# The first store of a pooling kernel in five pieces instead of one

## The chip, the cores and the metric

The kernel runs on one core of a Trainium2 chip. The metric is the time of one execution in microseconds, as the device measures it; before the change the median of three runs is 394.51 us (394.41 to 395.09). A profiled execution gives a trace, whose span begins and ends with the core's first and last instruction.

## The reference

The input `x` is 32 x 256 x 4096 in fp32, 134 MB. Along the last axis, each group of four neighbours gives one output, the root of the mean of the squares (an Lp pooling with p = 2 and kernel size 4); the output is 32 x 256 x 1024, 33.6 MB.

```python
for i in range(out_length):
    window = np.abs(x[:, :, 4 * i:4 * i + 4]) ** 2.0
    result[:, :, i] = (np.mean(window, axis=-1)) ** 0.5
```

## The kernel before

Both tensors are seen as flat. The input is cut into 20 loads of 128 partitions; loads 0 to 18 have W = 13184 values per partition (52,736 bytes), load 19 has 11648. Three tiles `x_tiles` take them in turn, so load i + 3 goes into the slot of load i. SP issues all loads (line 84): the first three at the start, then load i + 3 at the end of the work on load i.

The work on a load: ACT squares each half in place (`square`, line 98), DVE adds pairs (`pairs`, line 104) and then twos of these (`fours`, line 108) into one of two PSUM tiles `s_tiles`, and ACT takes the root of a quarter into `o_tile` (`root`, line 111). The order on ACT is by hand: the roots of load i - 1 stand between the two squares of load i.

Loads are grouped into blocks, [0, 1, 2, 3], [4, 5, 6, 7], [8, 9, 10, 11], [12, 13], [16, 17, 14, 15], [18] and [19], and a block is one contiguous stretch of the output. `o_tile` holds 4 x R values a partition, R = W / 4 = 3296, that is a block of four loads. There is one `o_tile`, so the roots of a block's successor wait until the block's store has landed. For this reason, where load i - 1 is the first of a block (i = 5, 9, 13, 17), both squares of load i come first, then the roots of load i - 1; DVE adds the pairs of both halves first and the fours, which need free PSUM tiles, last.

ACT issues the stores of blocks 0 to 3, right behind the last roots (line 95); SP issues those of blocks 4, 5 and 6 at the end. A store of a full block is one DMA of 128 partitions x 52,736 bytes.

At the very start ACT issues five tiny copies, one for each of the blocks 0 to 4 (`touch`, line 121): 128 values of every eighth partition's row from the input into the same rows of the block's output, which the block's store overwrites later.

Of the kernel before, what the change touches and what calls it, by code (L numbers as in the profile page):

```python
# [1 line left out]

# [4 lines left out]


@with_exitstack
def kernel(  # L10
    ctx: ExitStack,
    tc: tile.TileContext,
    x: bass.AP,
    p: float,
    kernel_size: int,
    out: bass.AP,
):

    nc = tc.nc

    assert float(p) == 2.0, "kernel specialized for p == 2"
    k = int(kernel_size)  # L30
    assert k == 4, "kernel specialized for kernel_size == 4"

    P = nc.NUM_PARTITIONS
    fp32 = mybir.dt.float32
    Act = mybir.ActivationFunctionType
    add = mybir.AluOpType.add
    xf = x.rearrange("b c l -> (b c l)")
    of = out.rearrange("b c l -> (b c l)")
    total = xf.shape[0] // P

    W = 13184
    H, R = W // 2, W // k
    X_SLOTS = 3
    TOUCH = 128
    LAST = total - 19 * W
    widths = [W] * 19 + [LAST]
    n = len(widths)
    assert 0 < LAST <= W and LAST % 16 == 0


    blocks = [[0, 1, 2, 3], [4, 5, 6, 7], [8, 9, 10, 11], [12, 13], [16, 17, 14, 15], [18], [19]]
    block_of = {i: b for b, loads in enumerate(blocks) for i in loads}
    block_width = [sum(widths[i] for i in loads) for loads in blocks]

    x_pool = ctx.enter_context(tc.tile_pool(name="x_pool", bufs=1))
    o_pool = ctx.enter_context(tc.tile_pool(name="o_pool", bufs=1))
    s_pool = ctx.enter_context(tc.tile_pool(name="s_pool", bufs=1, space=bass.MemoryType.PSUM))
    x_tiles = [x_pool.tile([P, W], fp32, name=f"xt{j}") for j in range(X_SLOTS)]
    o_tile = o_pool.tile([P, 4 * R], fp32, name="ot")
    first = o_pool.tile([P, 1], fp32, name="first")  # L60
    s_tiles = [s_pool.tile([P, 2048], fp32, name=f"st{j}") for j in range(2)]
    ctx.enter_context(tc.manual_schedule())

    def rows(flat, b, div):
        at = sum(block_width[:b]) * P // div
        return flat[at:at + block_width[b] * P // div].rearrange("(p w) -> p w", p=P)


    place = {}
    for b, loads in enumerate(blocks):  # L70
        for q, i in enumerate(loads):
            if i < 18:
                place[i] = o_tile[:, q * R:(q + 1) * R]
    free = x_tiles[17 % X_SLOTS]
    place[18] = free[:, 0:R]
    place[19] = free[:, R:R + LAST // k]

    xs = {}

    def load(i):  # L80
        b = block_of[i]
        at = sum(widths[j] for j in blocks[b][:blocks[b].index(i)])
        xs[i] = x_tiles[i % X_SLOTS][:, 0:widths[i]]
        nc.sync.dma_start(out=xs[i], in_=rows(xf, b, 1)[:, at:at + widths[i]])  # L84

    def store(b, queue):
        if b <= 2:
            held = o_tile[:, :]
        elif b == 3:
            held = o_tile[:, 0:2 * R]  # L90
        elif b == 4:
            held = o_tile[:, :]
        else:
            held = place[blocks[b][0]]
        queue.dma_start(out=rows(of, b, k), in_=held)

    def square(v):
        nc.scalar.activation(out=v, in_=v, func=Act.Square)  # L98

    def pairs(v):  # L100

        q = v.rearrange("p (n j) -> p n j", j=k)
        h = v[:, 0:v.shape[1] // 2].rearrange("p (n j) -> p n j", j=2)
        nc.vector.tensor_tensor(out=h, in0=q[:, :, 0:2], in1=q[:, :, 2:4], op=add)  # L104

    def fours(o, v):
        h = v[:, 0:v.shape[1] // 2].rearrange("p (n j) -> p n j", j=2)
        nc.vector.tensor_tensor(out=o, in0=h[:, :, 0], in1=h[:, :, 1], op=add)  # L108

    def root(o, s):  # L110
        nc.scalar.activation(out=o, in_=s, func=Act.Sqrt, scale=1.0 / k)  # L111

    def roots(i):
        for c in range(2):
            root(place[i][:, c * R // 2:(c + 1) * R // 2], s_tiles[c][:, 0:R // 2])
        if i in (3, 7, 11, 13):
            store(block_of[i], nc.scalar)

    def touch(b):
        to = rows(of, b, k)[0:P:8, 0:TOUCH]  # L120
        nc.scalar.dma_start(out=to, in_=rows(xf, b, 1)[0:P:8, 0:TOUCH])

    for b in range(5):
        touch(b)
    for i in range(X_SLOTS):
        load(i)

    nc.vector.memset(first[:, :], 1.0)  # L128
    root(first[:, :], first[:, :])
    for i in range(18):  # L130
        halves = [xs[i][:, c * H:(c + 1) * H] for c in range(2)]
        waits = i > 1 and (i - 1) % 4 == 0
        square(halves[0])
        if i and not waits:
            roots(i - 1)
        square(halves[1])
        if waits:
            roots(i - 1)
            for v in halves:
                pairs(v)  # L140
            for c, v in enumerate(halves):
                fours(s_tiles[c][:, 0:R // 2], v)
        else:
            for c, v in enumerate(halves):
                pairs(v)
                fours(s_tiles[c][:, 0:R // 2], v)
        if i + X_SLOTS < n:
            load(i + X_SLOTS)
    roots(17)


    c = 5560
    v = xs[18][:, 0:c]
    nc.vector.tensor_tensor(out=v, in0=v, in1=v, op=mybir.AluOpType.mult)  # L154
    square(xs[18][:, c:W])
    store(4, nc.sync)
    for a, b in ((0, c), (c, W)):
        pairs(xs[18][:, a:b])
        fours(place[18][:, a // k:b // k], xs[18][:, a:b])
    ends = [0, 6912, 10064, LAST]  # L160
    for a, b in zip(ends, ends[1:]):
        v = xs[19][:, a:b]
        o = place[19][:, a // k:b // k]
        square(v)
        if a == 0:
            root(place[18], place[18])
            store(5, nc.sync)
        pairs(v)
        fours(o, v)
        if a:  # L170
            root(*last)
        last = (o, o)
    root(*last)
    store(6, nc.sync)


# [1 line left out]
_INS = ['x', 'p', 'kernel_size']  # L178
_OUTS = [((32, 256, 1024), 'float32')]

_NUMBERS = {'p': 2.0, 'kernel_size': 4}


# [26 lines left out]
```

## Time and profile before

| | before |
|---|---|
| median of three runs | 394.51 us |
| profiled execution | 394.68 us |
| its span | 392.9 us |
| ACT busy | 279.3 us (71%) |
| DVE busy | 223.3 us (57%) |
| DMA moved | 167.83 MB, mean 427 GB/s |
| DMA queue 1 (SP) | 3312 packets, 144.15 MB |
| DMA queue 10 (ACT) | 736 packets, 23.67 MB |
| first store issued, landed | 90.15 us, 127.44 us |

Busy time is that in which an engine runs an instruction; instructions that issue DMAs aren't counted. The page cuts the span into 40 equal slices of 9.8 us and gives for each the mean busy share of the 16 DMA engines in tenths and the GB/s that they moved. Queue 1 is fed by SP, queue 10 by ACT, and both run on the same 16 DMA engines. A DMA row of the page gives the time from the issue to the landing, when its completion is signalled.

### The profile page before, as it was taken

Reading aid. Unit: us, or ns where it says so; the run is one execution under the profiler, and the core shown is the slowest. Engines: PE = TensorE matmul, PEld = TensorE weight load, DVE = VectorE, ACT = ScalarE, POOL = GpSimd, SP = SyncE. Lnnn points to the kernel's source line nnn. Section 1 sums busy time; section 2 is a strip of 40 time slices with the busy share of each in tenths; the row PEclk is TensorE's granted clock in tenths of the full one; section 3 lists DMA queues with packets and bytes.
Section 4 is the critical chain, followed back from the end, with each engine's and each line's share of the span. In section 5 each row is a group of like instructions: output and inputs, shape, how many; then the busy total and the mean of one; then the engine's idle time right before and its main releaser. Section 6 shows DMA issues by size and latency. Waiting matters only on the chain.

```text
span 392.9 us, 318 instructions
## 1 busy us (share of the span) xinstructions
DVE 223.3 (57%) x84; ACT 279.3 (71%) x82; POOL 0.2 (0%) x4
## 2 busy tenths in 40 slices
DVE  0046586666460568664606666645066654769992
ACT  1095988987650999886419898774297929897792
POOL 0000000000000000000000000000000000000000
DMA  8999999999999999999999999999999999999997
GB/s 344 432 430 430 430 430 435 456 440 387 430 430 430 430 430 440 435 451 435 440 430 431 440 430 435 435 435 430 435 430 419 440 430 430 430 434 446 425 423 320
DMA packets 4050, 167.83 MB, mean 427 GB/s; under 512 B 512, under 2 KB 592, under 8 KB 592
## 3 DMA queue, kind: packets, MB, share of 16 engines
q1 hardware_dynamic: 3312, 144.15, 85.3%
q10 hardware_dynamic: 736, 23.67, 13.9%
q14 instruction: 2, 0.02, 0.0%
HBM read 134.26 MB, written 33.60 MB: 427 GB/s over the span
## 4 chain that ended last, share of the span: by engine, by line
DMA 73%; ACT 17%; DVE 6%; issue 2%; SPq 0%; ACTq 0%; DVEq 0%
DMA xt<-in_x_dram 46%; DMA out_dram<-ot 27%; ACT xt L98 12%; ACT ot L111 5%; DVE xt L104 3%; DVE st L108 2%; DVE xt L108 1%; ACT xt L111 1%; SPq L84 0%; ACTq L98 0%; DVEq L104 0%; ACTq L111 0%
## 5 line engine op out<-in xcount | busy, mean ns | idle before, releaser
L98 ACT ACTIVATE xt<-xt 128x6592 f32<-128x6592 f32 (+4 forms) x40 | 221.4, 5547 | 58.5 <-DMA xt<-in_x_dram 56.8
L104 DVE TENSOR_TENSOR xt<-xt 128x3296 f32<-128x3296 f32 (+5 forms) x41 | 143.0, 3489 | 125.2 <-ACT xt L98 124.9
L108 DVE TENSOR_TENSOR st<-xt 128x1648 f32<-128x1648 f32 x36 | 67.4, 1882 | 36.2 <-ACT ot L111 34.3
L111 ACT ACTIVATE ot<-st 128x1648 f32<-128x1648 f32 x36 | 53.5, 1536 | 43.3 <-DMA out_dram<-ot 40.5
L108 DVE TENSOR_TENSOR xt<-xt 128x1390 f32<-128x1390 f32 (+4 forms) x5 | 7.3, 1452 | 0.2
L111 ACT ACTIVATE xt<-xt 128x3296 f32<-128x3296 f32 (+3 forms) x4 | 6.0, 1492 | 1.1 <-DVE xt L108 1.1
L154 DVE TENSOR_TENSOR xt<-xt 128x5560 f32<-128x5560 f32 x1 | 5.9, 5943 | 0.0
L111 ACT ACT_TABLE_LOAD x1 | 1.3, 1283 | 4.0 <-issue 4.0
L128 DVE MEMSET first<- 128x1 f32 x1 | 0.1, 59 | 0.8 <-PEq L191 0.8
L111 ACT ACTIVATE first<-first 128x1 f32<-128x1 f32 x1 | 0.2, 203 | 0.0
L191 POOL MEMSET const-bfloat16-1.0<- 128x1 bf16 x1 | 0.1, 102 | 0.0
L191 POOL MEMSET const-uint8-127<- 128x1 uint8 x1 | 0.1, 102 | 0.0
L191 POOL MEMSET const-float32-0.0<- 128x1 f32 x1 | 0.1, 99 | 0.2 <-issue 0.2
L191 POOL MEMSET const-float32-1.0<- 128x1 f32 x1 | 0.1, 99 | 0.0
## 6 DMA issues: line engine op xcount, KB each, us to landing
xt<-in_x_dram SPq DMA_DIRECT2D x19, 6592.0 KB, 33.6
out_dram<-ot ACTq DMA_DIRECT2D x3, 6592.0 KB, 35.2
out_dram<-ot SPq DMA_DIRECT2D x1, 6592.0 KB, 24.8
xt<-in_x_dram SPq DMA_DIRECT2D x1, 5824.0 KB, 25.2
out_dram<-ot ACTq DMA_DIRECT2D x1, 3296.0 KB, 27.4
out_dram<-xt SPq DMA_DIRECT2D x1, 1648.0 KB, 10.5
out_dram<-xt SPq DMA_DIRECT2D x1, 1456.0 KB, 5.8
out_dram<-in_x_dram ACTq DMA_DIRECT2D x5, 8.0 KB, 15.2
```

The source lines that it names most:

```text
L98: nc.scalar.activation(out=v, in_=v, func=Act.Square)
L104: nc.vector.tensor_tensor(out=h, in0=q[:, :, 0:2], in1=q[:, :, 2:4], op=add)
L108: nc.vector.tensor_tensor(out=o, in0=h[:, :, 0], in1=h[:, :, 1], op=add)
L111: nc.scalar.activation(out=o, in_=s, func=Act.Sqrt, scale=1.0 / k)
L128: nc.vector.memset(first[:, :], 1.0)
L154: nc.vector.tensor_tensor(out=v, in0=v, in1=v, op=mybir.AluOpType.mult)
L191: nc = _bacc.Bacc("TRN2", target_bir_lowering=False, num_devices=1)
```

## The change

The store of block 0 goes out as five DMAs, all issued by ACT in one go. Four take partitions 0 to 15: columns 0 to 824, 824 to 2472, 2472 to 5768 and 5768 to 13184, so 3.3, 6.6, 13.2 and 29.7 KB of each partition's row. The fifth takes partitions 16 to 127 with whole rows. Of the five tiny copies only that into block 4 is left. The other stores, the loads and the work on ACT and DVE stay as they are, in the same order.

```diff
         if i in (3, 7, 11, 13):
-            store(block_of[i], nc.scalar)
+            (store if i > 3 else ramp)(block_of[i], nc.scalar)
+
+    def ramp(b, queue):
+
+        cuts = [0, R // 4, 3 * R // 4, 7 * R // 4, 4 * R]
+        for a, e in zip(cuts, cuts[1:]):
+            queue.dma_start(out=rows(of, b, k)[0:16, a:e], in_=o_tile[0:16, a:e])
+        queue.dma_start(out=rows(of, b, k)[16:P], in_=o_tile[16:P, :])
...
-    for b in range(5):
-        touch(b)
+    touch(4)
     for i in range(X_SLOTS):
         load(i)
```

## The prediction

> **What bounds the kernel now.** I read the page's slices first, to see whether any engine or only the DMA is full.
>
> ```profile
> DVE 223.3 (57%) x84; ACT 279.3 (71%) x82; POOL 0.2 (0%) x4
> ...
> DMA  8999999999999999999999999999999999999997
> GB/s 344 432 430 430 430 430 435 456 440 387 430 430 430 430 430 440 435 451 435 440 430 431 440 430 435 435 435 430 435 430 419 440 430 430 430 434 446 425 423 320
> ```
>
> The 16 DMA engines are full from the first slice to the last, at 430 GB/s; ACT and DVE have slack. So a change gains or loses only what it adds to or takes from DMA time, idle DMA time included. In the trace's records of single DMA packets each 52,736-byte row of a load or store takes 1.947 us and the next starts 1.944 us after it, from 1.7 us to 391 us on every engine. Two places differ on every engine: its very first row (2.5 to 3.2 us), and one row per engine near 92 us, where slice 10 falls to 387 GB/s. Busy time in short windows there (window, length, engines' busy time, clock, DMA share, GB/s):
>
> ```profile
> 90.00:92.00 2.00, 1.90 (x2) 1.57 (x2) 0.00 (x0) 1.00 0.98 422
> 92.00:94.00 2.00, 0.87 (x1) 2.00 (x1) 0.00 (x0) 1.00 1.50 422
> 94.00:96.00 2.00, 0.00 (x0) 2.00 (x1) 0.00 (x0) 1.00 0.97 422
> ```
>
> Sixteen rows start in each window. Those of 92 to 94 us have a share of 1.50, so 3.0 us each instead of 1.95: the first store, issued at 90.15, costs every engine a stall of 1.06 us on average (0.54 to 1.76). The stores at 169.20 and 247.24 show none. This stall is what the change can win.
>
> Then the chain of waits around that store (start, length, what):
>
> ```profile
> 90.15 37.29 DMA out_dram<-ot
> ...
> 127.52 1.55 ACT ot L111
> ...
> 130.89 1.89 DVE st L108
> ...
> 132.79 27.73 DMA xt<-in_x_dram
> ```
>
> The roots of load 4 overwrite `o_tile`, so ACT waits until the whole first store has landed (127.44). Behind that stand the sums of load 5 and the issue of load 8 (132.79), which takes load 5's slot. Meanwhile loads 6 and 7 keep the DMA busy. How long? The timeline of ACT and DVE:
>
> ```profile
> 144.97 5.70 ACT L98 ACTIVATE xt<-xt 128x6592 f32<-128x6592 f32 x1 [0.43 <-DMA xt<-in_x_dram]
> 148.20 1.88 DVE L108 TENSOR_TENSOR st<-xt 128x1648 f32<-128x1648 f32 x1
> ...
> 160.60 5.70 ACT L98 ACTIVATE xt<-xt 128x6592 f32<-128x6592 f32 x1 [1.49 <-DMA xt<-in_x_dram]
> ```
>
> Load 7 lands at about 144.95, load 8 at 160.52. Load 9 is issued after the sum that ends at 150.08, which is 22.64 us after the store's landing, with no wait on a load between (ACT and DVE run back to back from 127.52). So a later landing of the first store delays loads 8 and 9 one for one, against a cover of about 12 and 10 us.
>
> Last, how small DMAs share the engines with loads: the tiny copies' time to landing.
>
> ```profile
> DMA to landing us min/median/max: 8.6/15.2/19.7
> ```
>
> They are issued 0.61 us apart from 0.73 on, so the first lands at 9.3 and the third at 17.2: 3.9 us per copy of 512 bytes a row, two load rows. The packet records show why: an engine takes the two queues in turn, and a DMA's completion is a packet of its own. The order is copy, load row, completion, load row, next copy.
>
> **Four tiny copies go.** Each costs an engine 24 + 6 ns (packet and completion), so 4 x 0.03 = -0.12 us. They need not be missed: the stores at 378 and 386 us go to parts of the output no tiny copy touched, and their rows run at 493 and 436 ns for a quarter of the bytes, without a stall. Their ACT issues (4 x 0.61) lay under ACT's 13.65 us wait for the first load.
>
> **Four more issues on ACT at 90.15.** At 0.34 (a store) to 0.61 us (a tiny copy) these are 1.4 to 2.4 us. Behind them on ACT stands the square of load 4's second half, then DVE's sums and load 7's issue (101.87 becomes 104.3 at most). ACT waits 5.55 us before 101.80 and load 7's first row has its turn near 129, so nothing shows; uncovered it would be 2.4 us. In the changed instruction order the second piece waits for the one tiny copy left (long landed), and loads 9 to 11 wait for pieces done some 50 us earlier: nothing.
>
> **The store lands later.** Per engine the store was 8 rows and a completion, 9 turns; between the first and the last lie 8 turns of the load queue, 7 rows and one load completion. Now it is four pieces, each with a completion, then 7 rows and a completion: 16 turns, with 15 load turns between, of which two are load completions. Bytes stored are equal, so the landing moves by 13 - 7 = 6 load rows: 6 x 1.944 = 11.7 us, to 139.1. Bytes are not lost by this, but the loads run out: load 8's issue moves to 144.4 and its first packet, 0.85 us later (the last store on idle engines: issued 386.24, first packets 387.1), to 145.3, against 144.6 when the slowest engine is done with load 7. Load 9 is issued at 161.7, first packet 162.6; load 8's last row ended at 160.2 before. Together the DMA loses 162.6 - 160.2 = 2.4 us. I take 2.3, since the slowest engines lose a little less. Load 10 (issue near 175.9, needed at 178.1) is in time again. The lag of ACT behind the loads, 9.7 us at load 8, shrinks by some 1.4 us a load, for ACT needs 14.15 us for a load that takes 15.55; store 1 goes out near 179, load 12 at 219.4 against 224.7 when the queue would be empty. Loads 18 and 19, and with them the end, keep only the 2.3 us.
>
> Bounds: if no engine is late with its first piece and the stall stays, the landing is 136.9 (the stores at 169.20 and 247.24 landed in 35.15 and 34.99 us, the first in 37.29) and load 9's first packet 160.4: about 0. A rerun of 37.29 gives 2.3. I take 2.3, the row of this very store.
>
> **What a piece costs.** No row shows 16 engines reading 16 neighbouring partitions. Lower bound: by bytes, 0.12 + 0.24 + 0.49 + 1.10 = 1.95 us, the row they replace, and the stall gone: -1.06. Upper bound: all eight row-equivalents of the store at the 3.0 us of the 92 us row: 8 x 1.06 = +8.5. I take the stall as it was plus one row at 3.0: +1.06, as the nearest row is a store's first. The 112-partition DMA I take as before, 7 rows an engine.
>
> [...]
>
> **Sum.** The profiled execution took 394.68 us, its span 392.9, 1.8 around it; the median of three runs is 394.51, so the steps are added to that: 394.51 - 0.12 + 2.3 + 1.06 = 397.7.
>
> **The rivals.**
> Rival 1, faster: the small pieces take the stall away and the loads do not run dry. It decides if the store lands by 160.2 - 0.85 - 22.64 = 136.7 or the alternation is looser than the tiny copies show. For it: the stall falls only on the first store, and the first piece is a sixteenth of a row. Against: the stalled row is a load's, before the store's first row, so its size may not matter. 394.51 - 0.12 - 1.06 = 393.3.
> Rival 2, no change: the change does not do what it says, the stall comes whatever the piece's size, and the landing is 136.9: 394.4 to 394.7.
> Rival 3, much slower: 16 neighbouring partitions, or 112 split by sevens, are read slowly at four to seven of the eight turns (+4.2 to +7.4), with the run-dry of 2.3: 401 to 404; without it 399.
>
> **How the numbers follow.** My forecast 0.43 (own range 395.4 to 399.5), rival 3 0.27, rival 2 0.15, rival 1 0.15. A measurement of this kernel can tell about 0.2%, 0.8 us. Faster is rival 1, 0.15; within 0.2% rival 2, 0.15; slower the rest, 0.70. The range runs from rival 1's 393.3 to five of eight slow turns with the run-dry, 394.4 + 2.3 + 5.3 = 402.0; above it lies about 0.08, and below it half of rival 1.
>
> **What would show it.** Right: the first store's last piece lands 46 to 50 us after the first issue; loads 8 and 9 are issued near 144 and 162; the DMA digits dip below 9 in the slices at 138 to 167 us and nowhere later; ACT's wait before the roots of load 4 grows from 14.4 to about 26 us. Wrong: a landing before 136 and full DMA slices there, or a drop of GB/s in slices 10 and 11 (rival 3), or a new stall at the stores at 169 or 247 us, which would mean that the tiny copies had a use.

## The result, and the profile after

The changed kernel took 407.65 us (median of four runs, 406.70 to 408.95), beside 394.68 us for the kernel before on the same chip: a ratio of 1.033, with an interval of 1.0318 to 1.0343. It is 13 us slower, and lies above the predicted range. The profiled execution took 407.37 us, its span is 405.6 us, 12.7 us longer than the span before.

The page's slices (DMA busy in tenths, GB/s) are read first:

```profile
DMA  8999999999899999999999999999999999999985
GB/s 339 458 447 421 416 432 468 432 421 402 347 421 374 406 411 416 416 432 406 400 411 416 444 442 411 426 395 421 421 421 419 468 424 426 421 447 450 431 371 219
```

Almost all digits are still 9: the DMA engines are as busy as before and move less. The low figures begin with 347 in slice 10, go on through 374, 406 and 411, come back at 406 and 400 (slices 18 and 19) and 395 (slice 26), and the end is thin (371, 219). So there isn't one lost stretch, there are four. Busy time in short windows (window, length, DVE, ACT, POOL busy, clock, DMA share, GB/s) shows the first two:

```profile
100.00:110.00 10.00, 6.50 (x4) 9.30 (x2) 0.00 (x0) 1.00 0.97 316
110.00:120.00 10.00, 2.92 (x1) 0.00 (x0) 0.00 (x0) 1.00 1.04 438
120.00:130.00 10.00, 0.00 (x0) 0.00 (x0) 0.00 (x0) 1.00 0.97 369
...
160.00:170.00 10.00, 7.37 (x4) 10.00 (x4) 0.00 (x0) 1.00 0.95 380
```

From 100 to 110 us, under the widest piece, the engines move 316 GB/s at a busy share of 0.97: rows take longer, nothing is idle. The fall to 347 in slice 10 is the sign that the prediction had set for rival 3. From 160 to 170 us load 9 comes late.

The chain that ended last (start, length, what) holds all three stores that ACT issues for full blocks:

```profile
90.54 48.67 DMA out_dram<-ot
...
178.90 39.85 DMA out_dram<-ot
...
258.44 39.30 DMA out_dram<-ot
```

The first store lands at 139.21 us. But the second and third store, which the diff doesn't touch, now land 39.85 and 39.30 us after their issue. Before it was 35.15 and 34.99; the second store then:

```profile
169.20 35.15 DMA out_dram<-ot
```

The timeline around the first store (start, length, engine, line, what, idle before and what ended it):

```profile
85.75 1.35 ACTq L123 DMA_DIRECT2D out_dram<-ot  x3
...
139.37 2.98 ACT L111 ACTIVATE ot<-st 128x1648 f32<-128x1648 f32 x2 [30.07 <-DMA out_dram<-ot]
140.95 3.67 DVE L108 TENSOR_TENSOR st<-xt 128x1648 f32<-128x1648 f32 x2 [28.02 <-ACT ot L111]
...
160.04 1.88 DVE L108 TENSOR_TENSOR st<-xt 128x1648 f32<-128x1648 f32 x1
```

Three of the pieces go out at 85.75 us, not at 90.15: their columns are ready before the last roots of the block. ACT's wait before the roots of load 4 is 30.07 us. The sums that end at 144.62 and 161.92 release loads 8 and 9.

Last, the trace's packet records, set out by engine. Against the normal time of a packet's size (1.947 us for 52,736 bytes) each stretch has an excess; the idle gaps are added, and the mean over the 16 engines is, in us:

| stretch | before | change | difference |
|---|---|---|---|
| 90 to 140 us (first store) | 1.05 | 4.83 | 3.78 |
| 140 to 180 us (loads 8 and 9) | 0.00 | 1.72 | 1.72 |
| 180 to 310 us (stores 2 and 3) | 0.17 | 4.20 | 4.03 |
| 310 us to the last packet | 0.95 | 4.23 | 3.28 |

The differences add up to 12.8 us, the 12.7 us of the span.

### The profile page after: what moved, and what is told of

Read it like the earlier page. It is cut to its first block, busy times and chain, and to the rows that moved or that the text cites. A ratio compares the mean times of both kernels' runs of the same rounds, so it can differ in the third digit from the quotient of the medians.

```text
span 405.6 us, 321 instructions
## 1 busy us (share of the span) xinstructions
DVE 223.4 (55%) x84; ACT 278.6 (69%) x82; POOL 0.2 (0%) x4
## 4 chain that ended last, share of the span: by engine, by line
DMA 61%; ACT 29%; DVE 5%; issue 3%; ACTq 0%; SPq 0%; DVEq 0%
DMA out_dram<-ot 32%; DMA xt<-in_x_dram 29%; ACT xt L98 20%; ACT ot L111 8%; DVE xt L104 3%; DVE st L108 1%; DVE xt L108 1%; ACT xt L111 1%; ACTq L123 0%; SPq L84 0%; ACTq L111 0%; ACTq L98 0%; DVEq L104 0%
```

## The experiments

Three theories were set against each other. A: a DMA over part of the partitions has slow rows, because of where these lie. B: the first store lands late, so the loads run dry. C: the 16 engines get out of step, and that costs time wherever loads and stores run together. Every run stands beside the kernel before on its own chip (394.6 to 394.8 us). The edits are shown in part: where the first store changes, the new lines take the place of the store of block 0.

### The tiny copies alone

```diff
-    for b in range(5):
-        touch(b)
+    touch(4)
```

> One part of the change alone: the tiny copies go from five to one, the first store stays one DMA. Theory A (the pieces' partitions: 16 engines reading neighbouring partitions serve each row slowly) and theory B (the pieces' completions only delay the landing of the store, and the loads run dry) both say 394.3 to 394.9 us, no difference. A third theory, that the missing tiny copies make the later stores stall, says a row of 3 us on every engine at the stores near 169 and 247 us, +1 us for each, 396 to 398.

Measured: 394.72 us beside 394.64, ratio 1.000 (0.9991 to 1.001); the stores landed after 37.06, 35.28 and 35.51 us. The copies are worth nothing either way.

### Partitions 0 to 15 and 16 to 127, whole rows

```diff
-            store(block_of[i], nc.scalar)
+        for a, e in ((0, 16), (16, P)):
+            queue.dma_start(out=rows(of, b, k)[a:e], in_=o_tile[a:e, :])
```

> The first store in two DMAs of whole rows, partitions 0 to 15 and 16 to 127, with five tiny copies. Turns of the store queue: 10 instead of 9, so the landing moves by one load row (1.9 us) by turns alone. Theory B: the loads do not run dry, 394 to 395 us. Theory A: the row of the 16 partitions takes 6 to 8 us instead of 1.95, some rows of the 112 take 2.3 to 4 us, the landing comes after 134 us, total 401 to 407.

Measured: 403.85 us, ratio 1.023 (1.0178 to 1.0283). The 16 rows of partitions 0 to 15 took 4.17 to 6.39 us each instead of 1.947. Nothing was split by columns here: two DMAs instead of one cost 9 us.

### Two halves, then even and odd

```diff
+        for a, e in ((0, 64), (64, P)):
+            queue.dma_start(out=rows(of, b, k)[a:e], in_=o_tile[a:e, :])
```

> The first store in two DMAs of 64 partitions each, whole rows, four rows an engine and DMA, with five tiny copies. Turns: 10, as with 16 and 112. Theory B: 394 to 395 us. [...]

Measured: 407.78 us, ratio 1.0326 (1.0308 to 1.0345), as much as the change. The counterpart takes the same two DMAs of 64 rows, with other partitions in each:

```diff
+        for a in range(2):
+            queue.dma_start(out=rows(of, b, k)[a:P:2], in_=o_tile[a:P:2, :])
```

> The two halves again, two DMAs of 64 whole rows each, but the even partitions (0, 2, ..., 126) and then the odd ones, instead of 0 to 63 and 64 to 127 (407.78 us). Number of DMAs, rows and bytes are the same, only which partitions stand in one DMA differs. [...] Theory A (placement of the partitions against the engines is the root of the slow rows, the late landing and the engines out of step): rows of 1.95 us, the first store lands 35 to 37 us after its issue, no engine more than 1.4 us behind, 394.3 to 395.5 us. Rival (any splitting into DMAs of fewer partitions does it, wherever they lie): 400 us or more, landing 40 us or later.

Measured: 395.85 us (median of 11 runs), ratio 1.0034 (1.0014 to 1.0054). Windows of the halves:

```profile
100.00:110.00 10.00, 4.99 (x3) 8.26 (x2) 0.00 (x0) 1.00 0.97 306
110.00:120.00 10.00, 4.65 (x2) 3.02 (x1) 0.00 (x0) 1.00 1.06 374
120.00:130.00 10.00, 0.00 (x0) 0.00 (x0) 0.00 (x0) 1.00 0.94 343
```

and of even and odd:

```profile
100.00:110.00 10.00, 5.20 (x3) 8.13 (x2) 0.00 (x0) 1.00 0.98 422
110.00:120.00 10.00, 4.78 (x2) 3.15 (x1) 0.00 (x0) 1.00 1.00 422
120.00:130.00 10.00, 0.00 (x0) 0.00 (x0) 0.00 (x0) 1.00 0.98 417
```

Same rows, same bytes, same number of DMAs: 306 to 374 GB/s against 417 to 422. Rows of the first store took 2.41 us on the mean in halves (63 of 128 over 2.05 us) and 1.98 in the other. This shows A for the halves: which partitions stand in one DMA is worth 12 of the 13 us, and splitting in two as such costs the remaining 1.2. With the partitions the rows of the output in one DMA change as well, and neighbouring rows there could be the cause instead. The copy on all 16 engines below speaks against that: it writes 16 neighbouring output rows of this length between load rows, and each took 1.95 us, where the first row of each engine from partitions 0 to 15 took 4.17 to 6.39.

### The four pieces alone, from 0 to 15 and from every eighth partition

```diff
+            queue.dma_start(out=rows(of, b, k)[0:16, a:e], in_=o_tile[0:16, a:e])
```

The second run has `0:P:8` in both places. The other 112 partitions of block 0 are not stored.

> The four pieces of partitions 0 to 15 alone; partitions 16 to 127 of the first block are left out of the output, seven rows an engine less: 394.7 - 13.6 = 381.1 us if the pieces cost nothing beyond their bytes. Theory A: the 29.7 KB piece takes 2.6 to 4.1 us again (1.1 by bytes), +2.4 us on the mean engine, 383.5. Theory C on top: the pieces leave the engines a row out of step, rows of 2.1 to 3 us in the later stores, 386 to 390.

> The same four pieces, but from every eighth partition (0, 8, ... 120) instead of 0 to 15; the other 112 partitions of the first block are left out. Base 381.1 us. [...] If the length of the pieces or their number is the cause and not the partitions, they take 2.6 to 4.1 us again. Time 381.1 to 385, below that of the pieces from 0 to 15.

Measured: 382.39 and 381.07 us. Seven rows an engine less are 13.6 us, so 381.2 would be no cost: the pieces cost 1.2 us from 0 to 15 and nothing from every eighth. The windows around the widest piece, from 0 to 15:

```profile
100.00:102.00 2.00, 1.72 (x1) 2.00 (x1) 0.00 (x0) 1.00 1.54 237
102.00:104.00 2.00, 0.68 (x1) 2.00 (x2) 0.00 (x0) 1.00 0.49 211
```

and from every eighth:

```profile
100.00:102.00 2.00, 1.92 (x2) 2.00 (x1) 0.00 (x0) 1.00 0.55 237
102.00:104.00 2.00, 0.60 (x1) 2.00 (x2) 0.00 (x0) 1.00 0.97 422
```

The share of a row counts where the row starts, so 1.54 is the 29.7 KB row made long: 3.08 us on the mean (2.56 to 4.04) against 1.10. The three narrower pieces took 129, 251 and 493 ns in both, their normal times.

### The 112 partitions alone

```diff
+        queue.dma_start(out=rows(of, b, k)[16:P], in_=o_tile[16:P, :])
```

Partitions 0 to 15 of block 0 are not stored.

> The first store takes only partitions 16 to 127 in one DMA; partitions 0 to 15 of the first block are left out of the output. That is one row an engine less (-1.9 us). Theory A with 112 partitions harmless and only the 16 narrow ones slow: 392.7. Theory A with both: rows of 2.2 to 4 us on some engines in this store. With theory C, slow rows at the later stores as well, 396 to 400.

Measured: 399.26 us (four runs, 397.82 to 401.88), where one row an engine less should give 392.7: this DMA alone costs 6.5 us. Only 12 of its 112 rows are over 2.05 us (up to 4.00), but afterwards the stores land after 39.91 and 40.14 us. No run stored these 112 rows from other partitions, so that their place is the cause here is argued from the halves.

### An early piece

```diff
+        if i == 0:
+            nc.scalar.dma_start(out=rows(of, 0, k)[:, 0:R // 4], in_=o_tile[:, 0:R // 4])
```

> All 128 partitions, but the first quarter of load 0's roots (824 columns, 3.3 KB a row) goes out alone right behind those roots at 43 us, and the first store takes the other 12360 columns. If the stall of 1.06 us near 92 us belongs to the size of a first store's rows, it goes: 393.4 to 393.8 us. If it belongs to the first store from SBUF whatever its size, it moves to 43 us and the time stays 394.4 to 394.9. Engines stay in step either way, and no row of 3 us follows.

Measured: 394.49 us beside 394.70, ratio 0.9994 (0.9984 to 1.0003). The stall near 92 us stayed (0.78 us an engine), and there was none at 46 us, where the early piece ran. So the stall does not come with a store's first packet as such, and a small first packet does not buy it off.

### Four DMAs of all partitions, by columns

Four equal quarters of the columns:

```diff
+        for a in range(0, 4 * R, R):
+            queue.dma_start(out=rows(of, b, k)[:, a:a + R], in_=o_tile[:, a:a + R])
```

> The first store in four DMAs of all 128 partitions, a quarter of the columns each, with five tiny copies: many turns (36 instead of 9) and no narrow range of partitions. Theory A: quarter rows at the normal rate (0.49 us) and no cost of its own. Theory B: the store finishes only when loads 6 and 7 have run out, landing near 145 us; load 8 is issued near 150 and load 9 near 167.5, first packet 168.4 instead of 160.2, so about 402.5 us, with gaps on all engines near 145 to 151 and 167 us and rows of 1.95 us elsewhere. If neither decides, 394.5.

Measured: 401.23, 400.37, 394.43 and 401.01 us. The expectation was badly made: the roots of load 4 wait for the first quarter alone, so nothing ran dry. In the profiled run (401.23) one engine fell 4.5 us behind after 183 us, and at the third store the rows took 2.23 us on the mean. The run of 394.43 us has no profile, so what sets it apart isn't known, and these runs decide nothing between the theories.

Then the cuts of the change, over all partitions (`[:, a:e]` for the four widths):

> The first store in the same four growing widths of columns, but each DMA over all 128 partitions, with five tiny copies: the change without narrow ranges. Theory A and C: rows at their normal rate and engines in step, 393.5 to 395 us; if a straggling engine appears, as in three of four runs of the quarter columns, near 401. Theory B (more completions, later landing, loads run dry): the roots of load 4 need only the first three DMAs, so no run-dry, 394.5. If narrow ranges are not the cause, 402 to 408.

Measured: 399.68 us, ratio 1.0116 (1.0091 to 1.0141). All rows of the store ran at normal speed (1.10 us for 29.7 KB), the fourth piece landed 57.9 us after its issue, since each of its rows stood between whole load rows (1.95 us) while there were any, and the engines were idle 3.2 us around 163 us. The later stores landed after 35.05 and 35.60 us. The expectation that nothing runs dry was wrong: it counted only the roots of load 4, but those of load 5 write columns of the fourth piece and wait for it.

```profile
148.16 1.54 ACT L111 ACTIVATE ot<-st 128x1648 f32<-128x1648 f32 x1 [4.03 <-DMA out_dram<-ot]
```

This is B nearly by itself, 5 us: no slow rows in the store, and at the later stores no engine over 1.0 us behind the median.

### A late store

```diff
+            if i == 5:
+                pairs(halves[0])
+                root(first[:, :], xs[5][:, 0:1])
+                store(0, nc.scalar)
```

> The first store stays one DMA of 128 partitions, but is issued later: behind the pair sums of load 5's first half and one tiny root on ACT, near 106 us instead of 90. Theory B alone, the price of a late landing without narrow ranges: landing near 141.5, load 8 issued near 146.8 and load 9 near 164, first packet 165 instead of 160.2; 398 to 400 us, idle DMA on all engines near 145 to 148, rows of 1.95 us elsewhere. If a late landing costs nothing, 394.6; if it puts engines out of step as well, above 401.

(The store behind the roots of load 3 goes.) Measured: 406.28 us (403.41 to 408.98). Three runs then took the wait away: the roots of loads 4 to 7 stay in PSUM, so nobody waits for the first store to land.

```diff
+            o = place[i][:, c * R // 2:(c + 1) * R // 2]
+            if i in (4, 5, 6, 7):
+                o = s_tiles[c][:, 0:R // 2]
+            root(o, s_tiles[c][:, 0:R // 2])
```

> Control: the kernel before with the roots of loads 4 to 7 written in place, so that they wait for no store (block 1 is not stored). Before, the wait of 14.44 us of ScalarE ended with loads still queued, so it set nothing: 394.3 to 395.1 us. If it did set something, the time falls below 394 us.

> The late store, issued near 106 us instead of 90 us, with the roots of loads 4 to 7 in place so that they wait for no store (block 1 is not stored). If the late landing costs only by what waits for it, the loads never run dry and the time is 394.5 to 396 us. If a store at that place puts the engines out of step by itself, 398 us or more, with engines over 2 us behind at the second or third store.

> The change, with the wait behind it taken out: the roots of loads 4 to 7 are written in place (into PSUM) and not into the output tile, so nothing waits for the first store to land before the roots of load 8; the second store goes out at its place with old contents. What is left of the computation out: block 1 is not stored. If the late landing, through the loads that run dry, carries most of the 13 us, 397 to 400 us (394.7 + 4.8 of slow rows before 140 us - 1.05 of the stall of before = 398.5). If the slow rows and the engines out of step carry it, 402 to 406 us (398.5 + 4 in later stores + 3 at the end = 405.5), with the second and third store landing after 38 us or more, and no idle stretches of the engines at 145 and 163 us in either case.

Measured: the kernel before with it 394.69 us, ratio 1.0003 (0.9993 to 1.0012); the late store with it 394.78 us, 1.0003 (0.9994 to 1.0012); the change with it 403.42 us, 1.0225 (1.0208 to 1.0242). The late store, with the wait:

```profile
140.00:150.00 10.00, 3.67 (x2) 7.63 (x3) 0.00 (x0) 1.00 0.50 185
...
270.00:280.00 10.00, 3.92 (x2) 9.64 (x2) 0.00 (x0) 1.00 0.92 343
```

and without it:

```profile
140.00:150.00 10.00, 0.00 (x0) 5.37 (x1) 0.00 (x0) 1.00 1.01 438
...
270.00:280.00 10.00, 2.96 (x1) 0.00 (x0) 0.00 (x0) 1.00 1.05 454
```

With the wait the engines stand half idle at 140 to 150 us, and over 100 us later rows are slow (343 GB/s). Without it both are gone, so the whole loss of the late store is B and what B sets off. For the change the wait is worth 407.65 - 403.42 = 4.2 us. The other 8.8 us are there without it. The page of that run (DMA issues: KB of one, us to landing):

```profile
out_dram<-ot ACTq DMA_DIRECT2D x2, 6592.0 KB, 38.0
...
out_dram<-ot ACTq DMA_DIRECT2D x1, 5768.0 KB, 48.6
```

The first store is as late as in the change, no load is, and the later stores still take long.

### Engines out of step

An added DMA at the start copies rows from DRAM to DRAM: a whole row on eight of the 16 engines, on all 16, and a quarter of a row on eight. It stands ahead of the tiny copies, that of the quarter behind them; the edit shown is the first.

```diff
+    at = sum(block_width[:5]) * P // k
+    nc.scalar.dma_start(out=of[at:at + 16 * W].rearrange("(p w) -> p w", p=16)[0:16:2], in_=xf[0:16 * W].rearrange("(p w) -> p w", p=16)[0:16:2])
```

> The kernel before with one more copy at the start, 8 rows of 52,736 bytes from input to output memory (a place that a store overwrites at the end), one row on each of eight engines, so that these run one row (1.95 us) behind the other eight. SBUF partitions and the first store are as before. Theory A (only narrow ranges of partitions cost): the later engines end one row later, 396.6 us, rows 1.95 us. Theory C (engines out of step slow each other while loads and stores run together): rows of 2.1 to 3 us during the stores, lags that grow beyond one row, 398 to 403.

> Control of the eight-engine copy: 16 rows, one on every engine, twice the bytes, all engines in step. Theories A and C alike: one row more, 396.4 to 396.9 us, rows of 1.95 us.

> The run with an added row on eight engines again, with a quarter of the row: an extra DMA at the start copies eight rows of 13.2 KB from DRAM to DRAM, one on each of eight engines, so that these eight are 0.5 us behind the others instead of 1.95 us. The bytes are worth 0.25 us of each engine, on the mean. If loads and stores slow each other once engines differ by more than about one row (1.95 us), nothing is lost here: 394.7 to 395.4 us, later stores landing after 34 to 36 us. If any difference between the engines costs time in proportion: about a quarter of the 4.5 us of the whole row, 395.6 to 396.5 us, and store landings above 36 us.

Measured: 398.70 us on eight engines (median of five runs, 397.0 to 401.24, ratio 1.0102, 1.0072 to 1.0133; two more took 404.31 and 404.4 and are left out of both), 396.57 on all 16 (1.0046, 1.0031 to 1.0061), 395.02 for the quarter (1.001, 1.0001 to 1.002). Half the bytes cost over twice the time. A window of the second store, with the row on eight engines:

```profile
180.00:200.00 20.00, 11.46 (x4) 11.28 (x2) 0.00 (x0) 1.00 1.01 411
```

and on all of them:

```profile
180.00:200.00 20.00, 9.40 (x4) 11.28 (x2) 0.00 (x0) 1.00 1.04 448
```

This shows C: a difference of about a row between the engines, set at the start and far from any store, makes rows slow 170 us later. It fits nearly all profiles. For the second and third store of the 20 profiles that I set out by engine I took how far the slowest engine is behind the median when all have begun the store, and the mean row of the 33 us that follow. In 24 cases no engine was over 1.5 us behind, and the mean row was 1.947 to 1.963 us. In 16 cases one was over 1.7 us behind; in 15 of these the mean row was 1.99 to 2.26 us, in one 1.959 us.

### The change with its sets spread

```diff
+            queue.dma_start(out=rows(of, b, k)[0:P:8, a:e], in_=o_tile[0:P:8, a:e])
+        for r in range(1, 8):
+            queue.dma_start(out=rows(of, b, k)[r:P:8], in_=o_tile[r:P:8, :])
```

> The change with its sets of partitions spread: the four growing pieces come from partitions 0, 8, ..., 120 instead of 0 to 15, and the other 112 partitions go in seven DMAs of sixteen partitions each, eight apart. Same bytes, same order of widths, more DMAs. Theory A (a DMA that takes neighbouring partitions makes several engines share what one engine serves in the whole store): the 29.7 KB rows take 1.10 us, the 52.7 KB rows 1.95 us, the first store lands by 127 to 129 us, no engine falls behind by more than 1.4 us, and the time is 394.0 to 396.0 us. Rival (the number of pieces, each with its own completion, costs the time): the first store lands after 132 us, and the time is 398 us or more.

Measured: 410.42 us, ratio 1.0404 (1.0384 to 1.0424): far off, and for a reason that neither theory had. ACT's part of the timeline:

```profile
90.76 14.71 ACTq L124 DMA_DIRECT2D out_dram<-ot  x7
105.52 5.70 ACT L98 ACTIVATE xt<-xt 128x6592 f32<-128x6592 f32 x1 [15.32 <-DMA out_dram<-ot]
```

The issue of the seven DMAs held ACT for 14.71 us, the squares behind it came late, and from about 118 us the engines had no loads beside the store. Then its rows grew longer, and those that began from 123 to 130 us took about 4.0 us (3.3 to 4.1), 16 x 52.7 KB in 4.0 us or 211 GB/s. The pieces themselves and the rows before 118 us, which alternated with load rows, ran at normal speed (1.95 us a whole row), but the run as a whole tells nothing of A against its rival. Even and odd, above, was made to tell them apart.

## Why the prediction was wrong, step by step

**Right.** The tiny copies: nothing (394.72 us beside 394.64). The landing of the first store: predicted 139.1, measured 139.21 us, though partly by luck: three pieces went out 4.4 us earlier than I had it, and the slow rows used that up. The issues of loads 8 and 9: 144.4 and 161.7 predicted, 144.62 and 161.92 measured. The sign "46 to 50 us after the first issue" holds only from the last issue (48.67); from the first, at 85.75, it is 53.5. ACT's wait: about 26 us predicted, 30.07 measured, since the squares of load 5 began at 98.02 us instead of 101.80. The direct loss at loads 8 and 9: 2.3 predicted, 1.72 measured, but only partly for the reason given: I had the engines idle, and only 0.37 us of it is idle time. The slow engines still had work when loads 8 and 9 were issued; the rest is long rows (up to 3.7 us), most of all the first of a load. So it showed as low GB/s (380 at 160 to 170 us) more than as the dips of the DMA digits that I named.

**Rival 1 had a true part.** The stall at 92 us did shrink. The window that had a share of 1.50 before:

```profile
92.00:94.00 2.00, 0.91 (x1) 2.00 (x1) 0.00 (x0) 1.00 1.03 422
```

That is worth under 1 us, and is inside the 3.78 us of the first stretch.

**Failed: what a piece costs.** I took one long row, +1.06 us on top of the stall. The 29.7 KB piece took 3.50 us on the mean in the change (2.65 to 4.07) where 1.10 is normal: +2.4. The narrower pieces, at 0.13, 0.25 and 0.49 us, cost nothing.

**Failed: "The 112-partition DMA I take as before, 7 rows an engine".** Its rows took 2.14 us on the mean, 27 of 112 over 2.05 us and up to 4.10: 7 x 0.19, another 1.35 us an engine. Alone it made a kernel 6.5 us slower than its bytes allow. Rival 3 had named "112 split by sevens" as the cause; its price for this (+4.2 to +7.4) was near the 3.78 us measured before 140 us.

**Failed: the end of the chain of reasoning.** "Loads 18 and 19, and with them the end, keep only the 2.3 us" is the step that cost most. Taking the two mis-sized terms at their measured size gives 394.5 + 3.8 + 1.7 = 400.0 us. The other 7.3 us of the profile (4.03 + 3.28) lie after 180 us, in stores that the diff doesn't touch. They are in no term of the sum and in no rival, Rival 3 included. Slow rows fell on some engines and not on others, so when the first store had landed the engines stood between 3.0 us behind the median and 2.5 us ahead, in the kernel before 0.8 and 0.3. While loads 8 and 9 came late the fast ones had to wait (0.37 us on the mean of all), and at the issue of the second store the slowest was 2.0 us behind, at that of the third 5.8. From the second store on rows were slow again (4.03 us), and at the end the engines that were done waited for the last rows of the others (3.28 us). No run took the unevenness alone out of the change; that it causes this is read from these figures and from the copies at the start. The runs without the wait say how much of it the late landing causes: 4.2 of 13 us with all that follows from it, and 8.8 come from the slow rows and what follows from them.

**The set of partitions.** The four pieces took 4.4 us in the change instead of 1.95, and only the widest was slow. The pair that decided took 407.78 us with halves and 395.85 us with even and odd partitions. Beside load rows the rows of a half took 2.41 us on the mean, those of every eighth partition 1.95; with no loads beside them the latter took about 4.0 us, 211 GB/s over the 16 engines. No trace records the way that a packet takes from its partition, so it is not shown why one set is slow and another isn't; that the set of partitions is the cause is shown for the halves and for the widest piece.

**Open.** Why rows are slow where engines differ by about a row (1.99 to 2.26 us on the mean in 15 of 16 cases) is not shown; neither the placement of the partitions nor the number of rows differs there from before. The slow rows fall on some engines and not on others: in the 33 us of the change's second store four engines lost 4.1 to 4.7 us each, the other twelve at most 1.8. Nor is it shown what first sets an engine back where all were in step: in the late store and in the quarter columns none was over 1 us behind as the second store began, at the third one was 2.9 and 4.6 us. The origin of the stall at 92 us is open as well. No version here beats the kernel before: the early piece is the same within its interval, and even and odd is 1.2 us slower.

## What to carry to other kernels

Where the DMA engines are the bound, the price of a DMA is not just its bytes: here DMAs over runs of neighbouring partitions were slow (rows of 2.41 us on the mean in halves) and spread sets, beside load rows, were not (1.98 in even and odd), and the loss didn't end with that DMA: 7.3 of the change's 12.8 us lie after 180 us. When costing an edit of this kind, ask whether it is even over the 16 engines; an uneven delay of about a row (1.95 us here) cost time in later stretches where loads and stores share the engines (4.0 us in all with a row on eight), an even one cost only its own bytes (1.9 us) in the one run that tried it. If a store must be split, keep every piece spread over the partitions, count one load row (1.95 us here) for each of its rows in the landing, look who waits for that, and keep the DMAs few: of eleven issues in a row the last seven held ACT for 14.71 us.

## What the runs showed of the hardware

- A row added at the start on eight engines cost more (398.70 us) than a row added on all sixteen (396.57 us).
- With two DMAs of 64 rows for the first store the kernel took 12 us more when they were halves than when they were even and odd partitions (407.78 and 395.85 us).
- ACT's issue of seven DMAs of 16 rows, behind four pieces, took 14.71 us and held the squares behind it; the change's five took 2.1 us (1.35, 0.32 and 0.44).
- Rows of every eighth partition took 1.95 us while they alternated with load rows, and up to 4.1 us with none beside them.
